# Sliding-window and dilated attention in head pairs: scores on both row halves, normalised P, values with v stationary

## The chip, the cores and the metric

The kernel runs on one core of a Trainium2 chip. The metric is the device time of one execution in microseconds (us), as the median of several runs.

## The reference, cut to what matters

Five layers follow each other on 256 tokens of width 1024. The first block has four layers; each is a mixer, a cross attention to a memory of 256 tokens and a convolutional gated feed forward, with a layer norm after each. The mixers are sliding-window attention with sinks (layers 0 and 3), a gated linear recurrence (1) and latent attention (2). The second block adds retention and dilated attention, an MLP and a gate. The change touches the sliding-window and the dilated attention:

```python
def swa_sink_attention(x, w_qkv, sinks, w_o, cos, sin):      # 16 heads of 64, 4 kv heads, blocks of 128
    q, k, v = jnp.split(x @ w_qkv, [...], axis=-1)            # q and k rotated
    scores = jnp.einsum('bnqhgd,bnkhd->bnhgqk', qb, kb) * (A_HEAD_DIM ** -0.5)
    scores = jnp.where(valid, scores, NEG)                    # a band of 128 keys back from the query
    probs = jax.nn.softmax(jnp.concatenate([scores, sink], axis=-1), axis=-1)[..., :-1]
    out = jnp.einsum('bnhgqk,bnkhd->bnqhgd', probs, vb)
    return out.reshape(bsz, s, A_HEADS * A_HEAD_DIM) @ w_o

def dilated_attention(q, k, v, pos):                          # 3 groups of 8 heads of 64
    for g, (window, dilation) in enumerate(((128, 1), (512, 4), (2048, 16))):
        o, l = dilated_group(q[:, :, sl], k[:, :, sl], v[:, :, sl], window, dilation)
    w = jax.nn.softmax(jnp.stack(lses, axis=0), axis=0)       # groups merged by softmax denominators
    return jnp.sum(w[..., None] * jnp.stack(outs, axis=0), axis=0)
```

Merging the three groups of a slot by their denominators is the same as one softmax over the keys of all three groups, and the kernel computes it so.

## The kernel before, in words

The 256 tokens are two token tiles of 128 (t = 0, 1). Activations lie transposed in SBUF as two f32r parts, high and low (`xTh`, `xTl`), and every weight is split into the same two parts when it arrives (`Cols.get` L108, `split` L201: a copy on ScalarE, a subtraction on VectorE). A product with weights is three f32r matmuls, high by high, high by low and low by high (`mm_nat` L209, lines 216 to 218). The attention products themselves are plain f32 matmuls.

Work is written down by a Python program, and a planner orders it when the kernel is built: the order in which instructions are written is their priority, and an instruction that the planner takes to be ready may pass one that is not. The result is a fixed order for each engine. PSUM has eight banks, handed out by tag (`PS_BUFS` L72): two `acc`, two `sc`, two `tr`, one `po`, one `tq`. SBUF work tiles also have tags (`S_BUFS` L71), four buffers each of `e`, `q`, `p` and `pT`.

`Skew` (L133) makes a pipeline of units. A unit has three parts: `scores`, `turn` and `values`. `unit` writes the scores of a unit, then `step` writes the turn of the unit before, one piece of other work (`fill`), and the values of the unit before that.

Sliding-window attention (`swa`, L616) first projects keys and values of a token tile (`kv`, L627) and queries of a token tile and half of the heads (`q`, L636). k^T is held twice, on partitions 0 to 63 and 64 to 127, and q^T holds the even heads of a pair on the first 64 partitions and the odd ones on the last 64. `attn(t, c, qT)` (L646) handles eight heads in units of `group(i0, par)` (L656): `nh` heads of one parity, four in token tile 0 (128 keys) and two in tile 1 (256 keys). `scores` (L660) multiplies on one row half (`r0`), adds the mask, takes the maximum with the sink and forms the exponentials with their sums. `turn` (L679) transposes P with TensorE through a `tr` bank, and ScalarE copies it out. `values` (L684) has P^T as the stationary operand, 128 by 128, and 64 columns of v stream by; all eight heads go into one `po` bank. `finish` (L697) divides by the sum, transposes o (four transposes) and splits it into `oTh` and `oTl`. For layer 0 the projections of the memory (`memkv`, L371) are the `fill`. The output projection (`out_proj`, L317) is written after the mixer.

Dilated attention runs over four slot pairs `sp`. `dil_proj` (L1111) projects keys, queries and values of two slots in three groups (six heads), and `dil_attn` (L1150) has, for each token tile, one unit a slot (`slot(h)`, L1161): scores of the three groups into `sc` banks, in tile 1 as two parts (groups 0 and 1, then group 2), mask, maximum, exponentials; the turn of P; the values with P^T stationary, accumulated over groups and key tiles into a `po` bank; and a `finish` (L1205) for both slots with one transpose of o. One `Skew` runs through all four slot pairs, so that the later parts of a pair are written behind the projections of the next.

Of the kernel before, what the change touches and what calls it, by code (L numbers as in the profile page):

```python
# [33 lines left out]
# 2*pi in three parts of at most 12 bits, and the rest  # L34
# [18 lines left out]
# Order of emission. An output projection runs token tile 0 ahead of tile 1 by LAG k-slices, and the  # L53
# last SPLIT slices of a tile one column half after the other.
# [28 lines left out]
class Cols:  # L83
    """Weight columns [K*128, ncol], loaded and split into exact high and low parts on demand."""
# [6 lines left out]
    def load(self, k):  # L91
        """the transfer of the k-slices around k"""
# [29 lines left out]
class Cat:  # L122
    """Tiles of four k-slices each, indexed as one."""
# [9 lines left out]
class Skew:  # L133
    """Emits units of three parts in a pipeline (the first part of a unit, then the second of the
    one before and the third of the one before that), and other work in between."""

    def __init__(self):
        self.a, self.b, self.fill = None, (), iter(())
# [6 lines left out]
    def then(self, f):  # L145
        self.a[1].append(f)
# [19 lines left out]
class Net:  # L166
# [97 lines left out]
    def rsqrt(self, v, n, eps):  # L264
        """(v/n + eps) ** -0.5 for a [P,1] column"""
# [39 lines left out]
    def steps(self, K, lag, split):  # L305
        """(token tile, k, column half) steps: tile 0 leads by lag, and its columns end one half after the other"""
# [10 lines left out]
    def out_proj(self, cols, Th, Tl, tail, lag=LAG, split=SPLIT):  # L317
        K = cols.K
        acc, left = {}, [2 * K, 2 * K]
        for t, k, n in self.steps(K, min(lag, K), split):  # L320
# [4 lines left out]
            if not left[t]:  # L325
                tail(t, acc[t])

# [156 lines left out]
    def nat_chunk(self, ws, t, dst, func=AF.Copy):  # L484
        """natural [128, 512] projections of token tile t"""
# [130 lines left out]
    def swa(self, j, mp):  # L616
# [27 lines left out]
        sk, fill = Skew(), iter(() if j else self.memkv(mp))  # L644

        def attn(t, c, qT):  # L646
            nk = (t + 1) * P
            nh = 512 // nk
            nkt = t + 1
            mask = self.mask[:, 256 - nk : 256]  # L650
            den = self.tiny("den", [4, 2])
            nm = self.tiny("nm", [4, 2])
            snk = sinks[:, 8 * c : 8 * c + 8].rearrange("p (a b) -> p a b", b=2)
            po = []

            def group(i0, par):  # L656
                r0 = 64 * par
                sm = self.s("p", [nh, nk])

                def scores():  # L660
                    ps = self.ps("sc", (nh, nk))
# [920 lines left out]
```

## Time and profile before

| | |
|---|---|
| median of 3 runs | 2102.25 us (2101.89 to 2102.45) |
| profiled execution, span (no other time of it is given) | 2101.9 us |
| TensorE busy | 2074.5 us, 99% |
| VectorE busy | 1540.1 us, 73% |
| ScalarE busy | 1182.6 us, 56% |
| first mixer on TensorE | 10.6 to 129.3 us |
| fourth mixer on TensorE | 1097.5 to 1174.3 us |
| dilated slot pairs, first scores of each | 1476.1, 1511.1, 1549.7, 1588.3 us |

In the rows, PE is TensorE, PEld its weight loads, DVE VectorE, ACT ScalarE, POOL GpSimd. Names are phase and tag: `b0swa` and `b3swa` are the two sliding-window mixers, `b3mo` the output projection of the fourth, `dp1` and `da1` the projections and the attention of the second dilated slot pair. The chain of waits is followed back from the last instruction, so that its pieces do not overlap: a piece's time is what it takes on the chain. An instruction's own duration includes its way through the engine and overlaps with its neighbours'. One f32 product appears as two matmul records, a transpose and an f32r product as one. A form such as `64*128 64x256` is rows and columns of the stationary operand, then partitions and columns of the streaming one.

### The profile page before, as it was taken

The page shows a single profiled execution, that of the slowest core. Times are in us where ns is not written, and L with a number is a line of the kernel's source. Part 1 is how long each engine was busy: PE and PEld are TensorE (multiplying, and loading weights), DVE is VectorE, ACT ScalarE, POOL GpSimd, SP SyncE. Part 2 cuts the span into 40 slices and gives each one's busy share as a digit, 9 for nine tenths or more (in the row PEclk, how much of TensorE's full clock was granted, in tenths as well). Part 3 has the DMA queues.
Part 4 walks back from the last instruction along what each step waited for, and adds up shares of the span by engine and source line. Part 5 has one row for each costly group of instructions (what it writes and reads, how often), then busy time and mean ns, then how long its engine had stood idle before and what let it go on. Part 6 is the DMA issues. An engine that isn't in the chain of part 4 may idle for free.

```text
span 2101.9 us, 33492 instructions
## 1 busy us (share of the span) xinstructions
PE 2074.5 (99%) x12349; PEld 1822.4 (87%) x12349; DVE 1540.1 (73%) x2988; ACT 1182.6 (56%) x2360; POOL 39.8 (2%) x54
## 2 busy tenths in 40 slices
PE   8999999999999999999999999999999999999998
PEld 6988899887899987889987889998899888788897
DVE  7656887799697777689788778878656556576666
ACT  5644666596476546456556456565555444455544
POOL 0000000000000000000000000000000000000000
PEclk9999999999999999999999999999999999999999
DMA  7354665436466543565654446754535546556652
GB/s 262 109 166 134 210 208 184 159 135 231 141 202 198 169 159 120 172 206 180 188 160 130 152 126 213 223 178 129 143 106 183 183 161 192 186 188 206 195 182 80
DMA packets 236660, 359.84 MB, mean 171 GB/s; under 512 B 13904, under 2 KB 157392, under 8 KB 236496
## 3 DMA queue, kind: packets, MB, share of 16 engines
q1 hardware_dynamic: 236496, 357.71, 52.9%
q8 instruction: 97, 1.59, 0.3%
q14 instruction: 67, 0.55, 0.1%
HBM read 356.60 MB, written 1.05 MB: 170 GB/s over the span
## 4 chain that ended last, share of the span: by engine, by line
PE 91%; DVE 4%; ACT 2%; DMA 1%; issue 1%; POOL 0%; SPq 0%; DVEq 0%; POOLq 0%; ACTq 0%
PE mlp.acc L216 1%; PE mlp.acc L217 1%; PE mlp.acc L218 1%; PE b0f.acc L216 1%; PE b3f.tr L224 1%; PE b2f.acc L216 1%; PE b2f.acc L217 1%; PE b0f.acc L217 1%; PE b3f.sc L224 1%; PE b2f.tr L226 1%; PE b1f.tr L226 1%; PE b0f.tr L226 1%; PE b2f.sc L226 1%; PE b3f.tr L226 1%; PE b2f.tr L225 1%; PE b2f.tr L224 1%
## 5 line engine op out<-in xcount | busy, mean ns | idle before, releaser
L203 DVE TENSOR_TENSOR mlp.wl<-mlp.raw,mlp.wh 128x512 fp32r<-128x512 f32 x132 | 86.0, 687 | 56.2 <-ACT mlp.wh L202 55.3
L202 ACT ACTIVATE mlp.wh<-mlp.raw 128x512 fp32r<-128x512 f32 x132 | 75.8, 624 | 59.3 <-issue 25.8
L202 ACT ACTIVATE b2f.wh<-b2f.raw 128x512 fp32r<-128x512 f32 x132 | 77.4, 624 | 33.3 <-PE b2f.tr L225 11.9
L202 ACT ACTIVATE b1f.wh<-b1f.raw 128x512 fp32r<-128x512 f32 x132 | 77.5, 624 | 31.9 <-PE b1f.tr L225 11.8
L202 ACT ACTIVATE b0f.wh<-b0f.raw 128x512 fp32r<-128x512 f32 x132 | 77.4, 624 | 31.5 <-PE b0f.tr L225 11.4
L202 ACT ACTIVATE b3f.wh<-b3f.raw 128x512 fp32r<-128x512 f32 x132 | 77.3, 624 | 29.1 <-PE b3f.tr L225 10.3
L203 DVE TENSOR_TENSOR b2f.wl<-b2f.raw,b2f.wh 128x512 fp32r<-128x512 f32 x132 | 85.6, 686 | 8.2 <-ACT b2f.wh L202 6.3
L203 DVE TENSOR_TENSOR b1f.wl<-b1f.raw,b1f.wh 128x512 fp32r<-128x512 f32 x132 | 85.6, 686 | 7.9 <-ACT b1f.wh L202 5.9
L203 DVE TENSOR_TENSOR b0f.wl<-b0f.raw,b0f.wh 128x512 fp32r<-128x512 f32 x132 | 85.5, 686 | 7.8 <-ACT b0f.wh L202 6.0
L203 DVE TENSOR_TENSOR b3f.wl<-b3f.raw,b3f.wh 128x512 fp32r<-128x512 f32 x132 | 85.6, 686 | 7.6 <-ACT b3f.wh L202 5.7
L224 PE MATMUL b3f.tr<-b3xo.xTh,b3f.wh 128*128 128x256 f32 x144 | 40.8, 283 | 0.0
L224 PE MATMUL b2f.sc<-b2xo.xTh,b2f.wh 128*128 128x256 f32 x144 | 40.8, 283 | 0.0
L224 PE MATMUL b0f.sc<-b0xo.xTh,b0f.wh 128*128 128x256 f32 x144 | 40.8, 283 | 0.0
L224 PE MATMUL b1f.sc<-b1xo.xTh,b1f.wh 128*128 128x256 f32 x144 | 40.8, 283 | 0.0
L224 PE MATMUL b3f.sc<-b3xo.xTh,b3f.wh 128*128 128x256 f32 x144 | 40.8, 283 | 0.0
L226 PE MATMUL b2f.tr<-b2xo.xTh,b2f.wl 128*128 128x256 f32 x144 | 40.8, 283 | 0.0
L226 PE MATMUL b0f.tr<-b0xo.xTh,b0f.wl 128*128 128x256 f32 x144 | 40.8, 283 | 0.0
L226 PE MATMUL b1f.tr<-b1xo.xTh,b1f.wl 128*128 128x256 f32 x144 | 40.8, 283 | 0.0
L226 PE MATMUL b3f.tr<-b3xo.xTh,b3f.wl 128*128 128x256 f32 x144 | 40.8, 283 | 0.0
L224 PE MATMUL b0f.tr<-b0xo.xTh,b0f.wh 128*128 128x256 f32 x144 | 40.8, 283 | 0.0
L225 PE MATMUL b0f.tr<-b0xo.xTl,b0f.wh 128*128 128x256 f32 x144 | 40.8, 283 | 0.0
L224 PE MATMUL b1f.tr<-b1xo.xTh,b1f.wh 128*128 128x256 f32 x144 | 40.8, 283 | 0.0
(1613 smaller groups left out, 7705.3 us busy)
## 6 DMA issues: line engine op xcount, KB each, us to landing
b0f.raw<-in_f_w_up_dram SPq DMA_DIRECT2D x44, 512.0 KB
b1f.raw<-in_f_w_up_dram SPq DMA_DIRECT2D x44, 512.0 KB
b2f.raw<-in_f_w_up_dram SPq DMA_DIRECT2D x44, 512.0 KB
b3f.raw<-in_f_w_up_dram SPq DMA_DIRECT2D x44, 512.0 KB
mlp.raw<-in_w_up_dram SPq DMA_DIRECT2D x32, 512.0 KB
mlp.raw<-in_w_down_dram SPq DMA_DIRECT2D x32, 512.0 KB
b0f.raw<-in_f_w_down_dram SPq DMA_DIRECT2D x22, 512.0 KB
b1f.raw<-in_f_w_down_dram SPq DMA_DIRECT2D x22, 512.0 KB
```

What stands on the lines that cost most here:

```text
L202: self.nc.scalar.activation(hi, src, AF.Copy)
L203: self.nc.vector.tensor_sub(lo, src, hi.bitcast(F32))
L216: mm(ps, Th[:, k, tok(t)], wh, start=start, stop=False)
L217: mm(ps, Th[:, k, tok(t)], wl, start=False, stop=False)
L218: mm(ps, Tl[:, k, tok(t)], wh, start=False, stop=stop)
L224: mm(ps, wh[:, cs], rh, start=start, stop=False)
L225: mm(ps, wh[:, cs], rl, start=False, stop=False)
L226: mm(ps, wl[:, cs], rh, start=False, stop=stop)
```

## The change

Two heads of a pair, one on each half of the array's rows, are one unit now. In sliding-window attention `group(i0)` takes both parities: their score matmuls alternate between partitions 0 to 63 and 64 to 127 and go into two `sc` banks. The sum with the sink and its reciprocal follow at once, and P is multiplied by it ahead of the transpose, the even heads by one VectorE instruction and the odd heads by ScalarE, one instruction a head. In `values`, v is the stationary operand (128 by 64) and P^T streams, two heads of a kv group together (256 columns); even heads are written to PSUM partitions 0 to 63 and odd ones to 64 to 127, alternating. What comes out is o transposed, and it is split straight into `oTh` and `oTl`; `finish` and its transposes are gone. Dilated attention is changed in the same way: both slots are one unit a token tile. In tile 1 the second part of the scores goes into the two `acc` banks and into one tile `pb` that holds both slots.

`step` writes the values of the unit two back first, then the turn, then `pieces` pieces of fill. In the fourth mixer both key projections come ahead of the queries, and the order of the heads changes; the first 16 steps of its output projection, which `out_steps` yields one by one, become the fill, three at a time. In layer 0 the last part of the memory projections is written two pieces at a time. Comments and docstrings are dropped as well.

```diff
 class Skew:
-        self.a, self.b, self.fill = None, (), iter(())
+        self.a, self.b, self.fill, self.pieces = None, (), iter(()), 1
     def step(self):
+        for f in self.b:
+            f()
         if self.a:
             self.a[0]()
-        next(self.fill, None)
-        for f in self.b:
-            f()
+        for _ in islice(self.fill, self.pieces):
+            pass
         self.a, self.b = None, self.a[1] if self.a else ()
...
     def swa(self, j, mp, mo):
...
+            def group(i0):
+                sms = [self.s("p", [nh, nk]) for _ in range(2)]
...
                 def scores():
-                    ps = self.ps("sc", (nh, nk))
+                    pss = [self.ps("sc", (nh, nk)) for _ in range(2)]
                     for x in range(nh):
-                        nc.tensor.matmul(ps[:, x], qT[r0 : r0 + 64, i0 + x, :], kT[r0 : r0 + 64, g, :nk],
-                                         start=True, stop=True)
+                        for par in range(2):
+                            r = slice(64 * par, 64 * par + 64)
+                            nc.tensor.matmul(pss[par][:, x], qT[r, i0 + x, :], kT[r, kv_head(x), :nk],
+                                             start=True, stop=True)
...
+                    nc.vector.tensor_add(es, nm, snk)
+                    nc.scalar.activation(es, es, AF.Exp)
...
+                    nc.vector.tensor_add(den, den, es)
+                    nc.vector.reciprocal(rd, den)
+                    nc.vector.tensor_mul(sms[0], sms[0], rd[:, 0, :, None].to_broadcast([P, nh, nk]))
                     for x in range(nh):
+                        nc.scalar.activation(sms[1][:, x], sms[1][:, x], AF.Copy, scale=rd[:, 1, x : x + 1])
...
                 def values():
+                    po = self.ps("po", (nh, P))
+                    for x in range(0, nh, 2):
+                        g = kv_head(x)
                         for kt in range(nkt):
-                            nc.tensor.matmul(po[0][:, h], pT[:, x, kt], v[:, kt, g * 64 : g * 64 + 64],
-                                             start=kt == 0, stop=kt == nkt - 1)
+                            for par in range(2):
+                                nc.tensor.matmul(po[64 * par : 64 * par + 64, x : x + 2],
+                                                 v[:, kt, g * 64 : g * 64 + 64], pTs[par][:, x : x + 2, kt],
+                                                 start=kt == 0, stop=kt == nkt - 1)
+                    self.split(po, oTh[sl], oTl[sl])
-            def finish():
...
-                nc.vector.tensor_mul(o, po[0], rd[:, :, None].to_broadcast([P, 8, 64]))
-                self.T_split(o.rearrange("p h d -> p (h d)"), oTh[sl], oTl[sl])
...
         kv(0)
         if j:
+            kv(1)
+            qa, qb = q(0, 0), q(0, 1)
+            units(0, 0, qa)
+            qa = q(1, 0)
+            units(0, 1, qb)
+            ua, ub = attn(1, 0, qa)
+            sk.unit(*ua)
+            qb = q(1, 1)
+            sk.fill, sk.pieces = islice(out, 2 * KD), 3
+            sk.unit(*ub)
+            units(1, 1, qb)
...
     def dil_attn(self, sp, qkv, yh, yl, sk):
...
+            tags = ("sc", "acc")
+            def scores():
...
+                for i, gs in enumerate(parts):
+                    pss = [self.ps(tags[i], (len(gs), nk)) for _ in range(2)]
+                    for x, g in enumerate(gs):
+                        for h in range(2):
+                            nc.tensor.matmul(pss[h][:, x], qT[rows[h], g, tok(t)], kT[rows[h], g, :nk],
                                              start=True, stop=True)
...
+                for i in range(len(parts)):
+                    nc.vector.tensor_scalar_mul(sms[0][i], sms[0][i], rd[:, 0:1])
+                    nc.scalar.activation(sms[1][i], sms[1][i], AF.Copy, scale=rd[:, 1:2])
...
+            def values():
+                po = self.ps("po", (P,))
+                for g in range(3):
+                    for kt in range(nkt):
+                        for h in range(2):
+                            pT = pTs[h][:, g, kt] if g < len(parts[0]) else pTs[2][:, h, kt]
+                            nc.tensor.matmul(po[rows[h]], v[:, kt, g * P + 64 * h : g * P + 64 * h + 64], pT,
+                                             start=g == 0 and kt == 0, stop=g == 2 and kt == nkt - 1)
+                self.split(po, yh[:, sp, tok(t)], yl[:, sp, tok(t)])
...
         for t in range(NT):
-            tile(t)
+            sk.unit(*tile(t))
```

## Rows read from the trace of the kernel before

**Rows 1.** The page: engines, and shares of the chain that ended last.

```profile
PE 2074.5 (99%) x12349; PEld 1822.4 (87%) x12349; DVE 1540.1 (73%) x2988; ACT 1182.6 (56%) x2360; POOL 39.8 (2%) x54
...
PE 91%; DVE 4%; ACT 2%; DMA 1%; issue 1%; POOL 0%; SPq 0%; DVEq 0%; POOLq 0%; ACTq 0%
```

**Rows 2.** Busy time by stretch: start:end, length, each engine, PEclk, DMA share, GB/s.

```profile
45.00:129.00 84.00, 84.00 (x550) 73.39 (x549) 52.38 (x112) 50.80 (x133) 0.00 (x0) 1.00 0.39 132
...
1122.00:1148.00 26.00, 26.00 (x157) 20.68 (x155) 21.84 (x52) 18.50 (x57) 0.00 (x0) 1.00 0.29 95
1148.00:1176.00 28.00, 27.93 (x169) 22.27 (x168) 17.01 (x47) 14.97 (x46) 0.00 (x0) 1.00 0.30 97
1511.00:1549.70 38.70, 38.70 (x238) 36.05 (x237) 22.72 (x66) 22.70 (x55) 0.00 (x0) 1.00 0.44 124
```

**Rows 3.** The chain of waits, fourth mixer, token tile 0: start, us on the chain, what.

```profile
1122.25 0.23 PE b3swa.acc L218
1122.47 1.64 PE b3swa.sc L664 x16
...
1130.89 1.08 PE b3swa.sc L664 x8
```

**Rows 4.** The chain of waits, fourth mixer, token tile 1 begins.

```profile
1142.39 1.06 PE b3swa.sc L664 x4
...
1144.04 0.84 PE b3swa.po L692 x8
1144.88 1.06 PE b3swa.sc L664 x4
1145.93 1.03 PE b3swa.po L692 x8
```

**Rows 5.** The chain of waits, second dilated slot pair.

```profile
1511.08 0.86 PE da1.sc L1170 x6
...
1512.75 1.29 PE da1.po L1199 x12
...
1516.38 0.63 PE da1.sc L1170 x2
...
1520.31 1.49 PE da1.sc L1170 x6
```

**Rows 6.** The chain of waits, first cross attention.

```profile
183.91 0.44 PE b0x.tr L258 x4
184.35 1.79 PE b0x.po L452 x16
```

**Rows 7.** Groups by form, 1097 to 1176, TensorE: count, busy us, mean ns, idle.

```profile
L692 PE MATMUL b3swa.po<-b3swa.v,b3swa.pT 128*128 128x64 f32 x96 | 12.7, 273 | 0.1
...
L664 PE MATMUL b3swa.sc<-b3swa.kT,b3swa.q 64*128 64x256 f32 x32 | 9.6, 408 | 0.0
...
L664 PE MATMUL b3swa.sc<-b3swa.kT,b3swa.q 64*128 64x128 f32 x32 | 4.0, 285 | 0.0
...
L258 PE MATMUL b3swa.tr<-ident,b3swa.q 128*128 128x128 f32 x16 | 2.5, 274 | 0.0
```

**Rows 8.** The same view, VectorE and ScalarE.

```profile
L666 DVE SCALAR_TENSOR_TENSOR b3swa.p<-b3swa.sc,mask 128x512 f32<-128x512 f32 x12 | 8.3, 688 | 3.5 <-PE b3swa.sc L664 2.2 <-PE b3swa.tr L258 1.2
L674 ACT ACTIVATE b3swa.p<-b3swa.p,b3swa.nm 128x256 f32<-128x256 f32 x16 | 7.9, 499 | 1.3 <-DVE b3swa.nm L672 1.3
L682 ACT ACTIVATE b3swa.pT<-b3swa.tr 128x512 f32<-128x512 f32 x12 | 7.1, 593 | 7.5 <-PE b3swa.tr L258 7.5
...
L674 ACT ACTIVATION_READ_ACCUMULATOR b3swa.p<-b3swa.p,b3swa.nm 128x1 f32 x32 | 6.1, 190 | 0.0
...
L669 DVE TENSOR_REDUCE b3swa.mx<-b3swa.p 128x2 f32<-128x512 f32 x8 | 5.3, 678 | 0.0
```

**Rows 9.** Timeline, TensorE: the first product of the fourth mixer.

```profile
1097.82 0.48 PE L216 MATMUL b3swa.acc<-b3swa.wh,b2f.xTh 128*128 128x512 f32 x1
```

**Rows 10.** Timeline, VectorE: the layer norm ahead of it, token tile 1.

```profile
1103.56 1.41 DVE L301 SCALAR_TENSOR_TENSOR x<-x,b2f.rs,b2f.vec 128x512 f32<-128x512 f32 x2
```

More of the change, by code (lines that the diff above doesn't have):

```diff
@@ L315, in steps, with out_proj, out_steps @@
         return out
-    def out_proj(self, cols, Th, Tl, tail, lag=LAG, split=SPLIT):
+    def out_proj(self, *a, **k):
+        for _ in self.out_steps(*a, **k):
+            pass
+    def out_steps(self, cols, Th, Tl, tail, lag=LAG, split=SPLIT):
         K = cols.K
@@ L326, in out_proj, with named @@
                 tail(t, acc[t])
+            yield
+    def named(self, phase, pieces):
+        while True:
+            was, self.phase = self.phase, phase
+            try:
+                next(pieces)
+            except StopIteration:
+                return
+            finally:
+                self.phase = was
+            yield
     def ln_tail(self, i, j, xT=True):
@@ L644, in swa @@
         sk, fill = Skew(), iter(() if j else self.memkv(mp))
+        order = ((0, 0), (1, 0), (0, 1), (1, 1))
         def attn(t, c, qT):
[L647 removed]
+            nkt = t + 1
+            nk = nkt * P
             nh = 512 // nk
[L649 removed]
             mask = self.mask[:, 256 - nk : 256]
[L651 to L654, printed above, removed]
@@ new lines, in scores @@
+                    mx, nm, den, es = (self.tiny(n, [2, nh]) for n in ("mx", "nm", "den", "es"))
+                    snk = sinks[:, heads].rearrange("p (a b) -> p b a", b=2)
+                    for par in range(2):
+                        nc.vector.scalar_tensor_tensor(sms[par], pss[par], 0.125,
+                                                       mask[:, None, :].to_broadcast([P, nh, nk]), ALU.mult, ALU.add)
+                        nc.vector.tensor_reduce(mx[:, par], sms[par], AX, ALU.max)
@@ L714, in swa, with units @@
+                    sl = (slice(None), slice(4 * c + i0, 4 * c + i0 + nh), tok(t))
+                    self.split(po, oTh[sl], oTl[sl])
+                return scores, turn, values
+            return [group(i0) for i0 in range(0, 4, nh)]
+        def units(t, c, qT):
+            for u in attn(t, c, qT):
+                sk.unit(*u)
+        out = mo(oTh, oTl)
         kv(0)
         if j:
-            qT = q(0, 0)
-            order = ((0, 0), (0, 1), (1, 0), (1, 1))
+            kv(1)
[9 more added lines that the diff above has]
+            units(1, 1, qb)
@@ L718, in swa @@
         else:
             self.x_xT(1)
-            order = ((0, 0), (1, 0), (0, 1), (1, 1))
-        kv(1)
-        if not j:
+            kv(1)
             qT = q(0, 0)
-        for n, tc in enumerate(order):
-            qn = q(*order[n + 1]) if n < 3 else None
-            if n == 1:
-                sk.fill = islice(fill, 2)
-            if n == 3:
-                sk.fill = fill
-            attn(*tc, qT)
-            qT = qn
+            for n, tc in enumerate(order):
+                qn = q(*order[n + 1]) if n < 3 else None
+                if n == 1:
+                    sk.fill = islice(fill, 2)
+                if n == 3:
+                    sk.fill, sk.pieces = fill, 2
+                units(*tc, qT)
+                qT = qn
@@ L732, in swa @@
         sk.rest()
-        return oTh, oTl
+        return out
     def lru(self, j, mp):
@@ new lines, in tile @@
+            rows = [slice(64 * h, 64 * h + 64) for h in range(2)]
+            first = [self.s("p", [len(parts[0]), nk]) for _ in range(2)]
+            sms = [[a] for a in first]
+            if t:
+                both = self.bp.tile([P, 2, nk], F32, tag="pb", name=self.nm("pb"), bufs=1)
+                for h in range(2):
+                    sms[h].append(both[:, h : h + 1])
+            def scores():
+                mx = self.tiny("mx", [len(parts), 2])
+                nm, rd = self.tiny("nm", [2]), self.tiny("rd", [2])
+                den = self.tiny("den", [len(parts), 2])
+                for i, gs in enumerate(parts):
[3 more added lines that the diff above has]
+                            nc.tensor.matmul(pss[h][:, x], qT[rows[h], g, tok(t)], kT[rows[h], g, :nk],
@@ L1215, in tile @@
-            for h in range(2):
-                sk.unit(*slot(h))
-            sk.then(finish)
+                    if i == 0:
+                        for h in range(2):
+                            nc.vector.tensor_reduce(mx[:, 0, h : h + 1], sms[h][0].rearrange("p g n -> p (g n)"), AX, ALU.max)
+                    else:
+                        nc.vector.tensor_reduce(mx[:, 1], both, AX, ALU.max)
+                        nc.vector.tensor_tensor(mx[:, 0], mx[:, 0], mx[:, 1], ALU.max)
+                nc.vector.tensor_scalar_mul(nm, mx[:, 0], -1.0)
@@ L1219, in dil_attn @@
+            return scores, turn, values
         for t in range(NT):
-            tile(t)
+            sk.unit(*tile(t))
     def gate_proj(self, sg, c0, b, tag, ptag):
```

129 lines of the change are left out of this document (43 added, 86 removed).

## The prediction

> **What bounds the kernel now.** I read the page first, then busy time by stretch, then the chain of waits inside the stretches that the change touches, then groups by form. The page shows TensorE busy 99% of the span and 91% of the chain that ended last [rows 1]; VectorE and ScalarE have 27% and 44% free. By stretch, TensorE is without a gap in all three places where the change lies: the first mixer (45 to 129 us), the fourth (1122 to 1176) and each slot pair of the dilated attention (38.7 us, one of four) [rows 2]. So a microsecond that leaves TensorE there leaves the span, as long as VectorE and ScalarE keep up: 52 and 51 of 84 us, 39 and 33 of 54, 23 and 23 of 38.7. PEclk is 1.00 in all of them, that is 2.4 GHz, so there is no clock to win back. DMA is at 0.29 to 0.44.
>
> In the chain, an f32 product counts as two matmul records (passes): a group of four heads in token tile 0 is x8, two heads in tile 1 x4. Passes of the scores use 64 rows of the array. Two bursts of one form give price and overhead: x6 takes 1.49 and x2 0.63 with 256 columns, so a pass is (1.49-0.63)/4 = 0.215 and getting in costs 0.63-0.43 = 0.20; with 128 columns x8 takes 1.08 and x6 0.86, so a pass is 0.11, and getting in again 0.20 [rows 3 to 5]. Getting out is paid by what follows: x8 value passes take 0.84 after full-array work and 1.03 after scores, 0.19 more [rows 4]. A burst of half-array passes thus costs 0.39 us beside its passes. That two row halves can run together is in the trace once: the x16 at 1122.47 holds both halves of a tile-0 group back to back in 1.64 us [rows 3], where one after the other would be 0.20+16x0.11 = 1.96. Three passes ran beside others.
>
> **The change part by part.**
>
> *Scores.* They alternate between row halves, product by product, into two PSUM tiles. Per sliding-window layer there are 32 passes of 128 columns and 32 of 256 [rows 7]: 3.52+6.88 = 10.4 us of passes, in 12 groups, 12x0.39 = 4.7; together 15.1. After: half the slots, 5.2, and six bursts. I add 0.11 to each burst of two halves, one pass in which the second half starts later (bounds 0 and 0.32, the part of the overlap seen): 6x0.50 = 3.0. Sum 8.2, gain 6.9 a layer. Per dilated slot pair: 12 passes of 128 and 12 of 256 columns, 3.9, in six bursts (x6, x6, x2, x2, x2, x6), 2.34: 6.2. After 1.95 and three bursts, 1.5: 3.45, gain 2.8.
>
> *Values.* Before, 96 passes a layer [rows 7] of 0.105 [rows 4], 10.1, with no change of the array's form. After, v (64 columns) is stationary and P^T streams: 48 passes of 256 columns. No pass with 64 stationary columns is in the trace. A pass with 128 streaming columns over full weights costs 1.79/16 = 0.11 [rows 6], so the price goes by the streaming columns and I take 0.215 at 256. If the two column halves run together: 24x0.215+6x0.50 = 8.2, gain 1.9 a layer. If not: 48x0.215+6x0.39 = 12.7, a loss of 2.6. Per slot pair 36 passes at 1.29/12 [rows 5], 3.9, become 18x0.11+2x0.50 = 3.0 (gain 0.9) or 36x0.11+0.78 = 4.7 (loss 0.8 to 0.9). I take the first: the row halves are shown to overlap, and two f32 streams together read no more columns a microsecond than one f32r product does (512 in 0.23 us [rows 3], twice the f32 rate).
> For columns there is a measured figure in the Trainium skill, "TensorE: Matmul & The Clock Gate", section "Part 3: Packing small matmuls — row/col tiling": three column tiles together gave 2.38 times. No run here shows it yet. Taken as 79% of ideal, an estimate from that page, the streaming slots would cost 24x0.215/0.79 = 6.5 a layer and 2.5 a pair, and the whole sum would be 4.8 us less good; its few nanoseconds between tiles would give back most of my 0.11 a burst.
>
> *Transposes of o.* These go: 16 a layer [rows 7] and 2 a slot pair, at 0.44/4 = 0.11 [rows 6]: 1.8 and 0.2.
>
> *Sum on TensorE.* A layer 6.9+1.9+1.8 = 10.6, twice 21.2; a slot pair 2.8+0.9+0.2 = 3.9, four times 15.6; together 36.8 us. With values one half after the other: 2x6.1+4x2.1 = 20.6.
>
> *What is added elsewhere.* P is normalised ahead of its transpose: one half by VectorE (about 0.69 for 512 columns, as the scaled mask [rows 8]), the other by ScalarE (bounds 0.30 and 0.50 a head, a 512-column copy without the read-out shared out over heads, and the exponential of 256 columns; I take 0.50). VectorE gains six of these and loses four multiplications of o, +1.4 a layer; ScalarE gets 8 copies in tile 0 and 8 in tile 1, 5 to 8 us a layer, and about 1.5 a pair. In the fourth mixer that makes VectorE and ScalarE some 40 us each of 54-10.6 = 43: they have little room left, and the chain of one unit is long. For tile 1: two masks 1.38, a reduction 0.68, four exponentials with their read-outs 4x0.69 = 2.76, two copies 1.0 [rows 8]: 5.8 before its first transpose, and 0.44+0.59 more to the first values, 6.8. TensorE has beside it the other units' 1.36+1.36+0.88 = 3.6, the next query projection (24x0.23 = 5.5 [rows 3]), in the first mixer the memory projections (those of the values alone 96x0.23 = 22), in the fourth 16 steps of the output projection, three a unit (0.69 each, 11 in all). In the three places that covers it, except at the end of the fourth mixer, where only leftovers of these steps stand beside the last unit: 1 to 4 us, I take 3. The 16 steps themselves are work that ran in this stretch before, so moving them is worth nothing. The two layer-norm vectors that are loaded with them move forward, with DMA at 0.30 [rows 2] to hide it. In the first mixer I take 1, in the dilated pairs 0.25 each: there the next 30 us of projections stand behind, but the second part of the tile-1 scores holds both "acc" accumulators, and the next projection behind them, until VectorE is through at most eight masks and reductions (8x0.69 = 5.5), against 8.4 of scores, turns and values. Bounds 0 and 2 a pair.
>
> *kv(1) ahead of the query projections* (fourth mixer). kv(0) begins at 1097.82 [rows 9] and is done 5.5 later, 1103.3; the layer norm of tile 1 delivers its first half at 1104.2 and its second at 1105.0 [rows 10], and transposing and splitting takes 1.6 more. Bounds 0 (query products of tile 0 are free to go first) and 2.6; I take 0.5.
>
> Waits 3+1+1+0.5, say 5. The profiled execution has a span of 2101.9 us and no other time; the median of the three runs is 2102.25, 0.35 above. 2101.9-36.8+5 = 2070.
>
> **The rivals.**
> *Column halves don't overlap.* For it: no row shows them. Against it: the example of the row halves, no more. 2101.9-20.6+4 = 2085.
> *VectorE and ScalarE become the bound.* ScalarE needs 2.76+1.0+2x0.59 = 4.9 us for a unit of tile 1 [rows 8], against 3.6 on TensorE: 1.3 too much where no projection stands beside it, and the 16 splits of the output weights fall into the same stretch. With all 12 units of both layers uncovered 16 us go, with ten microseconds more for the splits 26: 2081 to 2091, say 2088. Against it: 27 and 44% free on the whole. The Trainium skill, "TensorEngine Tiling (Array Packing)", section "PSUM Bottleneck", says that tiling speeds TensorE and not the emptying of PSUM, which may then bound; the 39 of 54 us of VectorE [rows 2] do not show it before the change.
> *Slower: the score buffers.* A unit takes both "sc" tiles, so the next unit's scores wait until VectorE has masked both, and the one "po" tile holds the next values until both splits have read it (0.59+0.69). The order on TensorE is fixed when the kernel is built, so whatever stands behind a waiting burst waits too. If that lays the chain of each unit bare, it costs 6.8-3.6 = 3.2 us, with the splits 4.5. It decides from 36.8/12 = 3.1 us a unit on; at 4.5 it gives 2101.9-36.8+54 = 2119. Against it: query projections of 5.5 us stand between most units.
> *It doesn't do what it says:* neither half overlaps. Then six bursts fewer a layer save 2.3 and values lose 2.6, the pairs save 1.2 and lose 0.9, and o's transposes give 1.8 and 0.2: 5 us in all, which the waits take back, 2102. Against it: 1.64 against 1.96 [rows 3].
>
> **How the numbers follow.** Forecast 2070, 0.53, by itself 2060 to 2078; columns apart 0.18; VectorE and ScalarE bound 0.14; score buffers 0.09; no overlap 0.06. Low end: no waits and no 0.11 on 44 bursts, 2101.9-36.8-4.8 = 2060, less one. High end: columns apart and 10 us of waits, 2091. That leaves out the slower case and the one without overlap, and little else. Within 0.2% (4 us, what a measurement of this kernel can tell from no change): no overlap, and a bit of the third case: 0.07; slower 0.09; faster 0.84.
>
> **What would show it.** Scores of one unit on the chain: x16 near 1.2 us where x8 was 1.08, and x8 with 256 columns near 1.2 where x4 was 1.06. Values x8 with 256 columns near 1.2 if the halves overlap, 1.9 if not. No transposes of o. A slot pair's 38.7 us come to 35, the stretch from 1122 to 1176 to 46 or so. It is wrong if TensorE shows idle time behind VectorE or ScalarE in the mixers of more than 5 us together, or if value bursts stand at 1.9.

## The result, and the profile after

Four runs of the changed kernel gave 2079.23 us in the median (2077.52 to 2082.66), four of the kernel before beside them 2102.22 (2101.89 to 2102.45): a ratio of 0.9891, 95% interval 0.9877 to 0.9906, 23.0 us less. The forecast was 2070, by itself 2060 to 2078, and its whole range 2059 to 2091: the median lies in the whole range and 1 us outside the narrow one. The profiled execution took 2078.6, of which 2076.8 are the span.

The page of the changed kernel, engines and shares of the chain that ended last, against [rows 1]:

```profile
PE 2040.2 (98%) x12213; PEld 1784.0 (86%) x12213; DVE 1539.4 (74%) x2972; ACT 1196.2 (58%) x2408; POOL 39.8 (2%) x54
...
PE 52%; DVE 3%; ACT 2%; DMA 1%; issue 1%; POOL 0%; SPq 0%; POOLq 0%; DVEq 0%; ACTq 0%
```

The last line can't be set against that of before: its shares add up to 59%, because the chain of the changed kernel could be followed back to 870 us of the span only.

TensorE's busy time fell by 34.3 us, near the 36.8 of the forecast's sum. The span fell by 25.1. So the time in which TensorE stands still rose from 2101.9-2074.5 = 27.4 to 2076.8-2040.2 = 36.6. The work went nearly as forecast, and 9 us of new waits came where the forecast had 5; the rest of this document looks for them.

First the work. The timeline of the changed kernel, TensorE, fourth mixer (start, duration with the way through the engine, records in a burst), against [rows 3, 4]:

```profile
1115.88 1.16 PE L681 MATMUL b3swa.sc<-b3swa.kT,b3swa.q 64*128 64x128 f32 x16
...
1128.93 1.13 PE L681 MATMUL b3swa.sc<-b3swa.kT,b3swa.q 64*128 64x256 f32 x8
1130.00 1.11 PE L718 MATMUL b3swa.po<-b3swa.pT,b3swa.v 128*64 128x256 f32 x8
```

Both kinds of halves overlap. Sixteen score passes take 1.16 where eight of one half took 1.08, eight of 256 columns 1.13 where four took 1.06, and the value burst, the shape that no row before showed, 1.11. Four slots of 0.215 and 0.20 to get in are 1.06. In the second dilated slot pair, the chain of waits of the changed kernel (start, us on the chain), against [rows 5]:

```profile
1497.87 0.87 PE da1.sc L1213 x12
1498.74 0.81 PE da1.po L1252 x12
...
1503.27 1.49 PE da1.po L1252 x24
```

Two x6 bursts of 0.86 became one x12 of 0.87. Busy time by stretch of the changed kernel (start:end, length, each engine, PEclk, DMA share, GB/s), against [rows 2]; its stretches start 8, then 13 us earlier:

```profile
45.00:60.00 15.00, 13.76 (x79) 9.47 (x78) 11.85 (x31) 12.72 (x49) 0.00 (x0) 1.00 0.41 140
60.00:129.00 69.00, 68.62 (x438) 57.13 (x437) 41.59 (x84) 45.57 (x114) 0.00 (x0) 1.00 0.52 167
...
1115.00:1141.00 26.00, 25.09 (x154) 18.20 (x153) 24.36 (x56) 21.80 (x73) 0.00 (x0) 1.00 0.32 101
1205.00:1217.00 12.00, 9.93 (x60) 9.19 (x60) 9.50 (x29) 4.77 (x14) 0.00 (x0) 0.86 0.52 175
1462.00:1476.00 14.00, 10.35 (x62) 9.20 (x61) 9.73 (x26) 8.51 (x23) 0.00 (x0) 0.88 0.46 129
1497.80:1532.30 34.50, 34.35 (x236) 32.15 (x235) 22.88 (x63) 23.93 (x57) 0.00 (x0) 1.00 0.49 137
```

The slot pair is 34.5 long (38.7 before, 35 forecast) and TensorE full in it. In the fourth mixer VectorE has 24.4 of 26 us, and TensorE stands 0.9. In 45 to 60, 1205 to 1217 and 1462 to 1476 TensorE stands 1.2, 2.1 and 3.7 us, and in the last two the granted clock is below 1.00: a mean of 0.88 over 14 us is 1.7 us of work lost, some 3.4 us at the lower of the two levels (1.2 GHz). The waits of TensorE (us in total, times, longest) that are new, four of them in these stretches:

```profile
PE dp1.acc L214 <- DVE da0.pb L1216: 2.7, 1, 2.7
PE b3x.po L467 <- DVE b3x.oTl L201: 2.1, 1, 2.1
...
PE b0swa.tq L256 <- DMA b0swa.e<-in_mem_dram: 1.2, 1, 1.2
...
PE da0.sc L1213 <- DVE da0.p L1216: 1.0, 1, 1.0
...
PE b3swa.tr L256 <- DVE x L299: 0.8, 1, 0.8
```

None of them stands in the same view of the kernel before; its fourth cross attention waits 1.3 us behind another instruction.

To see where a gain arises and is lost, the first product of each stage on TensorE is set against the same product before. The differences of these leads are the gain of a stage, in us. The fourth mixer counts up to the cross attention behind it, so its output projection is in it. The last column is the shortening of the whole span; small shifts in other stages make up the rest, and the forecast's 31.8 has its waits of 5.5 rounded to 5. Each row is one execution.

| kernel | first mixer | fourth mixer | fourth cross attention | dilated pairs | span |
|---|---|---|---|---|---|
| forecast | 9.6 | 7.1 | 0 | 14.6 | 31.8 |
| changed | 8.3 | 7.2 | -1.8 | 11.7 | 25.1 |
| a1_again | 4.8 | 7.0 | -0.2 | 11.3 | 22.7 |
| a2_tags | 5.1 | 7.2 | -1.6 | 14.9 | 25.2 |
| a3_step | 7.9 | 7.3 | 0.2 | 11.6 | 26.6 |
| a4_onehalf | 6.8 | 4.9 | -0.2 | 8.0 | 18.0 |
| b_both | 7.0 | 7.2 | -0.2 | 14.9 | 28.2 |
| b_valorder | 5.0 | 7.1 | 0.3 | 6.9 | 18.7 |
| b_nonorm | 8.6 | 9.5 | -0.1 | 12.0 | 28.7 |
| c_mem | 7.7 | 7.3 | 0.6 | 15.0 | 30.8 |
| c_mem2 | 7.0 | 7.3 | 0.0 | 15.0 | 29.2 |
| c_first | 10.2 | 7.3 | 0.6 | 15.0 | 33.8 |
| c_memkv | 7.5 | 8.6 | 1.3 | 15.0 | 32.9 |
| c_all | 10.1 | 8.6 | 0.0 | 15.0 | 34.1 |

### The profile page after: what moved, and what is told of

It is laid out like the page before. It is cut to its first block, busy times and chain, and to the rows that moved or that the text cites. A ratio compares the mean times of both kernels' runs of the same rounds, so it can differ in the third digit from the quotient of the medians.

```text
span 2076.8 us, 33251 instructions
## 1 busy us (share of the span) xinstructions
PE 2040.2 (98%) x12213; PEld 1784.0 (86%) x12213; DVE 1539.4 (74%) x2972; ACT 1196.2 (58%) x2408; POOL 39.8 (2%) x54
## 4 chain that ended last, share of the span: by engine, by line
PE 52%; DVE 3%; ACT 2%; DMA 1%; issue 1%; POOL 0%; SPq 0%; POOLq 0%; DVEq 0%; ACTq 0%
PE mlp.acc L214 1%; PE mlp.acc L215 1%; PE mlp.acc L216 1%; PE b3f.tr L222 1%; PE b3f.sc L222 1%; PE b2f.tr L224 1%; PE b2f.tr L223 1%; PE b2f.tr L222 1%; PE b3f.tr L223 1%; PE b3f.tr L224 1%; PE b2f.sc L224 1%; PE b3f.sc L224 1%; PE b3f.sc L223 1%; PE b2f.sc L223 1%; PE b2f.sc L222 1%; PE b2f.acc L214 1%
## 5 line engine op out<-in xcount | busy, mean ns | idle before, releaser
L200 ACT ACTIVATE b1f.wh<-b1f.raw 128x512 fp32r<-128x512 f32 x132 | 77.4, 624 | 32.8 <-PE b1f.tr L223 11.9
L200 ACT ACTIVATE b2f.wh<-b2f.raw 128x512 fp32r<-128x512 f32 x132 | 77.5, 624 | 32.2 <-PE b2f.tr L223 11.9
L223 PE MATMUL b1f.tr<-b1xo.xTl,b1f.wh 128*128 128x256 f32 x144 | 40.8, 283 | 0.0
```

The costliest lines, as they stand in the source:

```text
L200: self.nc.scalar.activation(hi, src, AF.Copy)
L223: mm(ps, wh[:, cs], rl, start=False, stop=False)
```

## The experiments

**a1_again**, the changed kernel once more. 

> The changed kernel as it is, beside the others of this batch: 2079 us, 23 less than before; it is the time that a2, a3 and a4 are set against.

2082.39 us (2080.94 to 2083.12), ratio 0.9906, interval 0.9892 to 0.9921. The two profiled executions differ by 2.4 us in their spans: the first mixer gained 4.8 in place of 8.3, 3.5 less, and the fourth cross attention lost 0.2 in place of 1.8. The same stretch, and the wait in it:

```profile
45.00:60.00 15.00, 12.94 (x54) 8.90 (x55) 10.87 (x27) 9.99 (x36) 0.00 (x0) 0.77 0.39 138
```

```profile
PE b0swa.tq L256 <- DMA b0swa.e<-in_mem_dram: 2.0, 1, 2.0
```

The wait for the memory's transfer was 2.0 here, and behind it the granted clock's mean is 0.77: 3.4 us of work lost. So these two executions differ by what this wait, and the clock behind it, happened to be.

**a2_tags**: other PSUM banks for the second part of the dilated scores.

```diff
-            tags = ("sc", "acc")
+            tags = (("sc", "sc"), ("tq", "po"))
...
-                    pss = [self.ps(tags[i], (len(gs), nk)) for _ in range(2)]
+                    pss = [self.ps(tag, (len(gs), nk)) for tag in tags[i]]
```

> The second part of the scores of token tile 1 in a dilated slot pair goes into one transpose bank and the value bank in place of the two projection accumulators. Theory (the accumulators held by VectorE are what took the first slot pair's gain): the 2.67 us that TensorE stands before the next pair's projection go, the 0.99 before the second part stays, and the 3.41 us at half clock behind it (some 1.7 us) go too: 4 us less than the changed kernel, 2075, nearly all in the first pair. Rival (TensorE waits for VectorE's masks there whatever bank is used, since the transposes behind stand in the same order): within 1 us, 2079.

2078.93 us (2076.69 to 2082.69), ratio 0.9893 (0.9878 to 0.9907). The interval overlaps that of a1_again, and the place in the trace decides. The first pair of the changed kernel, TensorE's timeline:

```profile
1462.70 0.94 PE L1213 MATMUL da0.sc<-dp0.B,dp0.C 64*128 64x128 f32 x12
1463.47 0.60 PE L1213 MATMUL da0.acc<-dp0.B,dp0.C 64*128 64x256 f32 x4
1465.06 1.59 PE L1213 MATMUL da0.sc<-dp0.B,dp0.C 64*128 64x256 f32 x8 [0.99 <-DVE da0.p L1216]
1469.32 0.66 PE L214 MATMUL dp1.acc<-dp1.wh,b3f.xTh 128*128 128x384 f32 x1 [2.67 <-DVE da0.pb L1216]
1469.77 0.52 PE L215 MATMUL dp1.acc<-dp1.wl,b3f.xTh 128*128 128x384 f32 x1
...
1472.24 0.34 PE L214 MATMUL dp1.acc<-dp1.wh,b3f.xTh 128*128 128x384 f32 x1
```

and that of a2_tags, with its busy time by stretch:

```profile
1467.14 0.45 PE L214 MATMUL dp1.acc<-dp1.wh,b3f.xTh 128*128 128x384 f32 x1
1468.20 1.59 PE L1213 MATMUL da0.sc<-dp0.B,dp0.C 64*128 64x256 f32 x8 [0.61 <-DVE da0.p L1216]
1469.72 0.44 PE L215 MATMUL dp1.acc<-dp1.wl,b3f.xTh 128*128 128x384 f32 x1
```

```profile
1462.00:1476.00 14.00, 13.39 (x86) 11.96 (x85) 10.36 (x24) 8.12 (x21) 0.00 (x0) 1.00 0.65 183
```

With the accumulators free the projection follows the scores at once, the clock stays at 1.00, and the pairs gain 14.9 in place of 11.3, 3.6 of the expected 4. The theory holds. In this execution the fourth cross attention, which the edit does not touch, took 1.4 of it away again (-1.6 against -0.2).

**a3_step**: cross and latent attention with the old order of a step (turn, fill, values).

```diff
-        sk = Skew()
+        sk = Skew(True)        # turn_first: the old order; in cross and in mla
```

> The cross and latent attention get the old order of a step back (turn, then fill, then values); the mixers and the dilated attention keep the new one. Theory (the new order costs the fourth cross attention an idle 2.07 us and the stretch at half clock behind it): 1.8 to 3.4 us less, 2076 to 2077, all of it between the fourth mixer's end and the fourth feed-forward. Rival (the shift comes from VectorE's angle computation, which meets the values in either order): within 1 us, 2079; or the other three cross attentions lose as much as the fourth wins.

2078.53 us (2077.05 to 2080.05), ratio 0.9889 (0.9874 to 0.9904). The fourth cross attention, the changed kernel, a1_again (the same kernel) and then a3_step:

```profile
1212.57 3.65 PE L467 MATMUL b3x.po<-b3x.pT,memv 128*128 128x128 f32 x16 [2.07 <-DVE b3x.oTl L201]
```

```profile
1216.14 2.02 PE L467 MATMUL b3x.po<-b3x.pT,memv 128*128 128x128 f32 x16 [2.09 <-DVE b3x.oTl L201]
```

```profile
1211.76 0.63 PE L261 MATMUL b3x.tr<-ident,b3x.p 128*128 128x128 f32 x4 [0.84 <-DVE b3x.p L456]
1212.54 2.05 PE L472 MATMUL b3x.po<-b3x.pT,memv 128*128 128x128 f32 x16
```

The new order puts values ahead of the turn, and they wait for a split on VectorE that has the angles' computation in front of it. In the changed kernel's first profile the granted clock is at its lower level behind this wait, and the sixteen products take 3.65; in a1_again they wait as long, the clock stays at 1.00, and they take 2.02. So of the 1.8 us that the stage lost in the first profile about 1.6 is the clock and 0.2 the order. Over all executions of the table, the new order gives -1.8 to 0.3 there (the two below -1.5 are those with the lower clock) and the old one -0.2 to 1.3, so the theory holds for the wait, and its price was that of one execution. The rival's other half, that the earlier cross attentions lose what the fourth wins, is wrong: by the same leads each of those three loses 0.2 to 0.6 in all six executions with the new order and nothing in the seven with the old one. That is 0.7 to 1.0 us in sum, which the fourth alone does not show. Most of the 3.9 us between the medians of a3_step and a1_again is the first mixer (7.9 against 4.8), which this edit does not touch.

**a4_onehalf**: all scores on one half of the rows, so that no rows overlap.

```diff
-                            nc.tensor.matmul(pss[par][:, x], qT[r, i0 + x, :], kT[r, kv_head(x), :nk],
+                            nc.tensor.matmul(pss[par][:, x], qT[:64, i0 + x, :], kT[:64, kv_head(x), :nk],
```

> All score products, of the sliding-window layers and of the dilated pairs, on array rows 0 to 63 (the odd heads' scores are taken from the even heads' data, so that part of the computation is changed); order, banks and bursts stay. Theory (the row halves run beside each other): the overlap's share comes back, 24 slots of 0.215 and 0.11 a layer = 5.2, twice, and 1.95 a dilated pair, four times: 18 us more, 2097; a burst of x16 with 128 columns 2.0 in place of 1.16, x8 with 256 columns 1.9 in place of 1.13. Rival (the gain is the fewer bursts, the transposes of o that went and the value products; the rows overlap little): 0 to 4 us more, 2079 to 2083.

2085.90 us (2085.69 to 2086.81), ratio 0.9925 (0.9909 to 0.9942): 3.5 above a1_again, not 18. The bursts behave as the theory says:

```profile
1118.48 2.05 PE L681 MATMUL b3swa.sc<-b3swa.kT,b3swa.q 64*128 64x128 f32 x16
...
1132.38 1.99 PE L681 MATMUL b3swa.sc<-b3swa.kT,b3swa.q 64*128 64x256 f32 x8
```

but their 5.2 a layer do not reach the span: 2.1 to 2.3 in the fourth mixer, and in the first 1.5 against the changed kernel's first profile, while against a1_again that mixer even gains 2.0 more. Counted from the start of each score product to the start of what follows it on TensorE, the fourth mixer's scores take 11.6 in place of 7.0, 4.6 more; TensorE stands 1.3 less there and the value products take 0.7 less. The first mixer's take 12.6 in place of 9.8, only 2.8 more, because the planner had broken some of its bursts apart (c_first shows them), so that part of the overlap was not there to lose. In the first mixer TensorE comes to the memory's transfer later and waits 0.3 for it:

```profile
PE b0swa.tq L256 <- DMA b0swa.e<-in_mem_dram: 0.3, 1, 0.3
```

That is 0.9 less than in the first profile: there a part of what the faster scores saved had gone into a longer wait. In a pair the overlap is worth 1.1, not 1.95: from start to start, scores take 1.53 more without it, but the values and transposes behind take 0.4 less. So what stands behind a burst is that much dearer when the burst used both halves; why is not shown. Theory and rival each held in part.

**b_both**: a2_tags and a3_step together. 

> Both edits at once: other banks for the second part of the dilated scores, and the old order of a step in the cross and latent attention. Theory (two causes in two places): the shifts add, 3.7 from the dilated pairs and 0.5 to 1.8 from the cross attention; 4 to 5.5 less than the changed kernel, 2077 where that gave 2082.4; no stretch at half clock at 1212 nor at 1464 to 1475. Rival (the waits are given back later, or the half clock only moves to another place): 2079, as with either edit alone.

2076.19 us (2075.49 to 2078.98), ratio 0.9875 (0.9860 to 0.9889). The pairs gain 14.9, as in a2_tags, and the three earlier cross attentions lose nothing, as in a3_step; so the edits add in that. The 0.5 to 1.8 forecast for the fourth cross attention did not come: it gives -0.2, as a1_again did. PEclk is 1.00 from 1205 to 1217 and from 1462 to 1476. In the first mixer it is 0.89 from 45 to 60, behind a DMA wait of 1.4.

**c_mem**, with it the memory's loads earlier, into the tile that holds the memory's values later.

```diff
                 qn = q(*order[n + 1]) if n < 3 else None
+                if n == 0:
+                    self.mem_load()      # the four loads that memkv issued, into memv
```

> As the kernel with both edits, and the loads of the memory in the first mixer are issued some 10 us earlier, into the tile that later holds the memory's values. Theory (the 1.2 to 2.0 us that TensorE waits there for a DMA are on the path, and the two stretches at half clock behind it are its doing): the DMA wait goes, PEclk is 1.00 from 48 to 60, and 1.5 to 5 us go, 2073 to 2075. Rival (TensorE waits there for VectorE and ScalarE next): within 1 us of the kernel with both edits.

2073.49 us (2072.85 to 2076.22), ratio 0.9864 (0.9847 to 0.9880), 2.7 less than b_both in the same batch. The wait and the lower clock go:

```profile
45.00:60.00 15.00, 15.00 (x82) 10.22 (x81) 13.58 (x35) 13.16 (x46) 0.00 (x0) 1.00 0.41 138
```

Still the first mixer gains no more than 7.0 to 7.7 (c_mem2 and c_mem), against 7.0 in b_both, under the forecast's 9.6 and under the changed kernel's own 8.3. So at its own place the edit is worth 0 to 0.7, not the 1.5 to 5 of the theory; the rest of the 2.7 lies in stages that it does not touch, 0.8 of it in the fourth cross attention. The wait was not all.

**b_valorder**: value products of one column half ahead of the other's.

```diff
-                    for x in range(0, nh, 2):
-                        g = kv_head(x)
-                        for kt in range(nkt):
-                            for par in range(2):
+                    for par in range(2):
+                        for x in range(0, nh, 2):
+                            g = kv_head(x)
+                            for kt in range(nkt):
```

> The changed kernel with the value products of one column half ahead of those of the other, in place of alternating. Theory (the halves run beside each other only where neighbours in the queue alternate): a value burst of x8 in a sliding-window layer 1.8 to 1.9 in place of 1.08, 4.8 a layer; in a dilated pair 18 slots of 0.11, 2 us. Half of the mixers' part comes through, as it did for the scores, all of the pairs': 4 + 7, some 10 us more than the changed kernel, 2090 (18 if all comes through). Rival (the array works ahead over the order, or the value gain is from the wider products): no change, and x8 stays near 1.1.

2084.54 us (2083.89 to 2085.56), ratio 0.9912 (0.9898 to 0.9927). The sliding-window bursts did not change, the dilated ones did (0.88 and 1.53 with halves alternating; one of 24 records is missing):

```profile
1133.34 1.11 PE L718 MATMUL b3swa.po<-b3swa.pT,b3swa.v 128*64 128x256 f32 x8
...
1501.06 1.15 PE L1252 MATMUL da1.po<-da0.pT,dp0.A 128*64 128x128 f32 x12
...
1505.86 2.35 PE L1252 MATMUL da1.po<-da1.pT,dp0.A 128*64 128x128 f32 x23
```

Four passes of one half and then four of the other still run side by side in 1.11; six and six take 1.15, between 0.88 and the 1.5 of no overlap at all (12x0.11 and 0.20). Against halves one after the other, 0.81 us is saved in the x8, 0.37 in the x12 and 0.49 in the x24, that is 3.4 to 4.5 passes each (at 0.215 a pass in the x8 and 0.11 in the others). By this estimate TensorE works ahead over about four passes, so alternating matters only where one half has more than that in a row. The pairs lose 4.4 against a1_again, four times the 0.27 and 0.82 of the two bursts, and the whole span 4.0; the theory was right for the pairs in kind, with 7 for 4.4, and wrong for the mixers, to which it gave 4. The rival was right there.

**b_nonorm**: P is not normalised.

```diff
-                    nc.vector.tensor_mul(sms[0], sms[0], rd[:, 0, :, None].to_broadcast([P, nh, nk]))
-                    for x in range(nh):
-                        nc.scalar.activation(sms[1][:, x], sms[1][:, x], AF.Copy, scale=rd[:, 1, x : x + 1])
```

> The changed kernel without the normalisation of P (the multiplications by the reciprocal on VectorE and the scaled copies on ScalarE are left out in the sliding-window layers and the dilated pairs, so the output is not the reference's); TensorE's instructions stay. Theory (in the mixers the chain of one unit over VectorE and ScalarE is part of the bound, which is why only half of the score overlap came through there): 3 to 5 us less than the changed kernel, from the two mixers, and 0 to 1 from the dilated pairs; 2078 where that gave 2082. Rival (it lies beside TensorE's work, and the mixers' waits are for the planner's order and a DMA): within 1 us.

2074.86 us (2074.74 to 2077.78), ratio 0.9869 (0.9854 to 0.9884). The fourth mixer gains 9.5 in place of 7.0 to 7.2: 2.4 us there are VectorE's and ScalarE's chain. The dilated pairs gain 12.0 against 11.3 to 11.7, and the first mixer 8.6, about the changed kernel's best. The theory holds for one mixer. Most of the rest of what this run is ahead of a1_again lies in the first mixer (8.6 against 4.8), where the wait for the memory was 1.0 here and the clock at 1.00 behind it.

**c_mem2, c_first, c_memkv and c_all**: what the two mixers still lack. c_mem2 is c_mem again, 2074.38 us (2073.08 to 2075.36), ratio 0.9863 (0.9849 to 0.9878).

> The kernel with both edits and the early loads of the memory once more, beside the next three: 2073 to 2074 us, 29 less than before.

c_first writes the scores of a unit ahead of the next query projection in the first mixer:

```diff
-                qn = q(*order[n + 1]) if n < 3 else None
...
-                units(*tc, qT)
-                qT = qn
+                us = attn(*tc, qT)
+                sk.unit(*us[0])
+                qT = q(*order[n + 1]) if n < 3 else None
...
+                for u in us[1:]:
+                    sk.unit(*u)
```

> As c_mem2, and in the first mixer the scores of a unit are written ahead of the next query projection, so the planner puts them first. Theory (the projections' higher priority breaks score bursts in the first mixer: x4 and x4 of one half each at 1.06, and an x16 in three pieces at 1.71 together, against 1.06 and 1.09 whole; that is the 2 us that the layer misses against the forecast): 1.5 to 2 us less, 2072, all of it ahead of 130. Rival (the bursts break where a bank is not free yet, whatever the priority, or the order is better for the scores and worse for the loads of the weights): within 1 us, or slower by up to 2.

2070.28 us (2069.88 to 2073.57), ratio 0.9848 (0.9833 to 0.9862): 4.1 less. TensorE's timeline in the first mixer, c_mem2 and then c_first:

```profile
48.37 1.13 PE L690 MATMUL b0swa.sc<-b0swa.kT,b0swa.q 64*128 64x256 f32 x4
50.71 1.13 PE L690 MATMUL b0swa.sc<-b0swa.kT,b0swa.q 64*128 64x256 f32 x4
...
59.31 0.71 PE L690 MATMUL b0swa.sc<-b0swa.kT,b0swa.q 64*128 64x128 f32 x6
60.97 0.49 PE L690 MATMUL b0swa.sc<-b0swa.kT,b0swa.q 64*128 64x128 f32 x2
61.97 0.72 PE L690 MATMUL b0swa.sc<-b0swa.kT,b0swa.q 64*128 64x128 f32 x8
```

```profile
45.96 1.14 PE L690 MATMUL b0swa.sc<-b0swa.kT,b0swa.q 64*128 64x256 f32 x8
...
49.01 1.13 PE L690 MATMUL b0swa.sc<-b0swa.kT,b0swa.q 64*128 64x256 f32 x8
...
57.35 1.16 PE L690 MATMUL b0swa.sc<-b0swa.kT,b0swa.q 64*128 64x128 f32 x16
```

In c_mem2 one unit's eight passes stand as two x4 of 1.13, each as long as a whole burst: the planner had sent one half without the other. An x16 stands in three pieces. In c_first all are whole, and the first mixer gains 10.2 in place of 7.0 (7.7 in c_mem). That is 2.5 to 3.2, more than the 1.5 to 2 that the bursts themselves explain; which of the moved projections gives the rest was not tried apart.

c_memkv puts the first query projection of the fourth mixer back ahead of kv(1):

```diff
-            kv(1)
-            qa, qb = q(0, 0), q(0, 1)
+            qa = q(0, 0)
+            kv(1)
+            qb = q(0, 1)
```

> As c_mem2, and in the fourth mixer the first query projection stands ahead of kv(1) as it did before the change. Theory (kv(1) ahead of the queries is what makes TensorE wait 0.8 us for the layer norm of token tile 1): 0.5 to 0.8 less, 2072.8. Rival (those transposes stand ahead of the projections in either order): 0.

2071.94 us (2070.79 to 2073.40), ratio 0.9854 (0.9838 to 0.9871). The wait of 0.8 for the layer norm no longer stands in the list, and the fourth mixer gains 8.6 in place of 7.3. The theory holds, with 1.3.

> Both: the sum of the two if each holds, 2071; it is the version that should beat all others.

c_all gave 2069.69 us (2067.73 to 2072.77), ratio 0.9843 (0.9828 to 0.9857), 32.8 us less than before: the two gains stand in its trace side by side (10.1 and 8.6), though its time cannot be told from that of c_first. It beats both kernels. TensorE is busy 2038.0 of a span of 2067.8, still for 29.8 us, close to the 27.4 of before.

## Why the prediction was right in its direction and 9 us short

*The terms on TensorE.* Right in sum. Busy time fell by 34.3 against 36.8, and some 1.7 of the difference is the clock: two stretches at the lower level lie in the changed kernel's profile (at 1212 and 1469) and one in that of before (at 473). In a pair, start to start, scores, values and transposes of the second slot pair went from 11.7 to 7.9 together, 3.8 against 3.9. The split among them was off: values gave 1.8 (forecast 0.9), scores 2.1 (2.8), and the transposes nothing; that part of what a burst costs to leave is paid by what follows would explain it, but is not shown. The doubtful step, that column halves overlap, holds: 1.11 for x8. For the page figure that stood against it, 2.38 times for three column tiles (the Trainium skill, "TensorE: Matmul & The Clock Gate", section "Part 3: Packing small matmuls — row/col tiling"), the trace shows another and better case: two halves at nearly the price of one (1.11 against 1.06).

*What is added elsewhere.* The fourth mixer's tail was put at 3 (1 to 4); taking the normalisation out gives 2.4 there, and the mixer gained 7.2 against 7.1. The rival in which VectorE and ScalarE become the bound is true in that one stretch and to that size. That 7.2 meets 7.1 so well is partly luck: the tail cost 0.6 less than its term and kv(1) 0.8 more. The rule of the section "PSUM Bottleneck" (the Trainium skill, "TensorEngine Tiling (Array Packing)") is not tested by this: what b_nonorm leaves out works on P in SBUF, and no run changes how PSUM is emptied there.

*The step that failed first* is "in the dilated pairs 0.25 each", with bounds 0 and 2. It named the right mechanism, the two accumulators held by the second part of the scores, and then covered it with "8.4 of scores, turns and values". In the first pair there are no turns and no values of a pair before. That pair gained -0.2 in place of 3.65, with 3.7 us of standing still (the two new waits above, 1.0 and 2.7) and 1.7 of lost clock; the other three gained 4.1, 4.1 and 3.6. Other banks gave 3.6 back.

*The second* is "in the first mixer I take 1", hidden by the memory projections. Those were there, but their first transposes wait for a transfer issued just ahead of them, 0.3 to 2.1 us in the executions that load it so late, with the clock at its lower level behind the longer ones, and the planner broke score bursts apart. Loading early and writing the scores first brought 10.2 of the 10.6 that the sum had on TensorE, nearly all of it with the second edit. Why the changed kernel's own 8.3 is above the 7.0 to 7.7 with the loads early stays open.

*The third was not in the text at all.* The new order of a step was costed in the two attentions that the change is about. The helper serves cross and latent attention too. In the first three cross attentions it is a loss of 0.7 to 1.0 us together, in every execution; in the fourth it lays a wait of 1.6 to 2.15 bare, which cost 0.2 or less, and 1.6 to 1.8 in the two executions where the clock fell behind it. In the latent attention no steady difference shows.

*kv(1)* was put at 0.5 and cost 1.3. *The clock:* "no clock to win back" was true of the stretches of before; that there was clock to lose was not asked. *The sum's base:* 2101.9 is a span, and the runs here take 1.8 us more than their span, so the profiled execution of before would have a time of 2103.7 (an estimate), 1.5 above the median. Between the two profiled executions the forecast is 6.7 short (31.8 against 25.1): 1.3, 1.8 and 2.9 from the first mixer, the fourth cross attention and the pairs make 6.0 of it. Between the medians it is 9.2 short (32.2 against 23.0), since the profiled execution of before was slower than its median by that estimate, that of the changed kernel was 0.6 faster, and the forecast's base lies 0.35 under the median.

## What to carry to other kernels

When work leaves the engine that bounds, ask of each repetition by itself what covers the waits behind it: the first pair, the first layer and the last unit have neighbours that the average one has not. Follow every caller of a helper whose order changes. Then compare busy time with span: if busy time falls as computed and the span does not, the list of waits that are new names the places, and moving a bank, a load or a line of the program may give the rest. Set the same place of several executions side by side before a wait is given a price: the same wait cost 0.2 in one and 1.8 in another.

## What the runs showed of the hardware

TensorE ran passes of two column halves side by side although four passes of one half stood ahead of the other's (1.11 either way), and ran them partly apart with six ahead (1.15 against 0.88). The x16 of [rows 3], 1.64 with eight and eight, fits that.

Inside the program the granted clock fell to its lower level only where TensorE had just stood still, but not wherever it had. From 45 to 60 the mean granted clock was 1.00 in the executions where the wait for the memory's transfer was 0.3, 1.0, 1.1 and 1.2 us (a4_onehalf, b_nonorm, a3_step, the changed kernel), 0.89 at 1.4 (b_both) and 0.77 at 1.8, 2.0 and 2.1 (a2_tags, a1_again, b_valorder). From the execution with 1.2 to that with 2.0 the first mixer's gain fell by 3.5 us.

At other places the length of the wait does not decide. In the fourth cross attention the clock fell behind waits of 2.07 and 1.93 us (the changed kernel, a2_tags) and stayed at 1.00 behind 2.09, 2.15, 2.06 and 1.64 (a1_again, a4_onehalf, b_nonorm, b_valorder). In the second layer's output projection TensorE waits 1.9 us for a split of the weights in every kernel, that of before too; the clock fell behind it in ten of the fourteen profiled executions and stayed in four (the changed kernel, a1_again, b_both, c_first). The wait, and busy time in the 12 us around it, before and then changed:

```profile
PE b1mo.acc L216 <- ACT b1mo.wh L202: 1.9, 1, 1.9
```

```profile
471.00:483.00 12.00, 9.81 (x36) 7.11 (x35) 12.00 (x21) 9.18 (x16) 0.00 (x0) 0.86 0.51 173
```

```profile
PE b1mo.acc L214 <- ACT b1mo.wh L200: 1.9, 1, 1.9
```

```profile
463.00:475.00 12.00, 9.35 (x39) 6.77 (x38) 12.00 (x21) 9.11 (x16) 0.00 (x0) 1.00 0.51 178
```

What decides there is not shown. Eight runs of one kernel spread over 2077.5 to 2083.1; such stretches are the likely reason, but only two of the eight were profiled.
